# Bias columns to ScalarE, one square sum to VectorE, one sum for half of the first scale, and a new order of all instructions

## The chip, the cores and the metric

The kernel runs on one core of a Trainium2 chip. A core has a matrix engine (PE, TensorE; its weight loads are listed apart as PEld), a vector engine (DVE, VectorE), a scalar engine (ACT, ScalarE), a general engine (POOL, GpSimd) and an engine that issues DMAs (SP, SyncE). Each engine works through a stream of its own in the order in which the program gives it, and waits by semaphores for the others. PE writes its results to PSUM, a memory of eight banks on 128 partitions; DVE and ACT carry them from there to SBUF. The metric is the device time of one execution in microseconds.

## The reference

One layer of a hybrid decoder, 1024 tokens of width 1024, all in float32. What the change touches is marked.

- A modulation vector `c` gives shift, scale and gate columns: `silu(c) @ w_mod + b_mod`. The first **scale** multiplies the normalized `x` before the input projection.
- One input projection `x_mod @ w_in` gives q, k, v, z of four heads (128 columns each) and the inputs lx and gates ly of the recurrent group (four tiles of 128 columns each). The shift enters as a bias: a **column** `shift @ w_in` is added to every token.
- The heads run a chunked gated delta rule: a triangular system per chunk of 64 tokens is solved, then a state is carried from chunk to chunk.
- The recurrent group convolves lx, makes two gates from it (`r`, `i`), then

```
a = exp(8 r log_sigmoid(lam));  b = sqrt(max(1 - a^2, 1e-12)) * (i * x)
h = scan(h = a*h + b);          y = gelu(ly) * h
```

  and `y` is divided by its root mean **square** over the 512 channels of the group.
- Output projection with residual, then an MLP `relu(h @ w_up)^2 @ w_down` with its own norm, scale and shift, and a last norm.

## The kernel before

All matrices that matter for accuracy are split into a high and a low part (names end in `h` and `l`), and a product is three matmuls: high by high, high by low, low by high. A matrix of 1024 x 128 weights is kept as `<name>_w`, split by ACT (CAST to `<name>_wh`) and DVE (difference to `<name>_wl`).

The stages on the time axis of the profile, as the traces of their tiles lie: the first scale, the norm of `x` and the k projection (0 to about 80 us), then the z, q and v projections, which are woven in among the triangular systems (80 to 230), the chunk recurrence of the four heads with the lx and ly projections (180 to 345), the recurrent gates (310 to 414), the output projection (about 385 to 460), the MLP (485 to 1107), and the last norm.

`Proj` makes one projection tile: `third(i)` runs the matmuls of tokens 0 to 511, 512 to 767 or 768 to 1023 into PSUM tiles `<name>_p0`, `_p1` and `_p2`. `_p2` has two columns more, one of which is the bias column of the tile (column 256). That column is copied to `<name>_b` first (line 678), and then ACT empties each third with it as its bias (Identity for q, v, lx; Silu for z; Gelu for ly) into `<name>_st`. `Key` (k0 to k3) is made in another way, and copies its bias column by itself (line 710).

ACT has a table for each family of functions, and an ACT_TABLE_LOAD stands in its stream where the next function needs another one; the wait of the instruction behind it can stand on the load itself.

The triangular systems: `gc` (Gram products, brought into rows by ACT copies) is multiplied on DVE by `bcoef`, which needs `rnk`, a reciprocal root of `ssk` that POOL computes as a power; the product is transposed to `gg`, and 62 DVE steps on `xx` and `ftmp` build the inverse of 32-row blocks. The transposed results `xnc` and `xtc` feed the PE products `it`, `iy`, `iw` and `iz`.

`lru(ct, ...)` is the recurrent group's tile ct: `gate<ct>..` are PE products of the convolved input xr (split to `xrh` by ACT and `xrl` by POOL, for ct 3 by DVE), ACT takes tanh of them (`ta`, `ti`), exp (`aa`), tanh and square (`a2`), DVE multiplies and clips (`ta`), ACT takes the root, DVE scans, multiplies with the gate into `ly<ct>_st`. Its square (`lsq`) is added to `msum` on POOL; after ct 3, PE sums `msum` over partitions (`lrus`), and by way of a DVE transpose, a POOL power and a trip through DRAM (`lnd`, `lrus_b`) the norm comes to `lcm`, which is split to `lch` and `lcl` for the second half of the output projection (`wl`). `wg` is its first half, over the heads; DVE carries its PSUM tiles to `x1`.

What sets the order: the program first records every operation without issuing it. `emit` (lines 323 to 337) then issues them in the order of a table `ORDER` (unpacked from a text at the head of the file), and gives each tile the buffer that a second table, `SLOTS`, names; so line 336 stands for all instructions but the grouped matmuls of line 462. Nothing else orders the streams. SBUF and PSUM tiles are reused under waits that follow from the two tables.

Of the kernel before, what the change touches and what calls it, by code (L numbers as in the profile page):

```python
# [106 lines left out]
def dram_box(ap):  # L107
# [12 lines left out]
    'qo#TL)E!oz1rw7A@7#3r&)>vNyY8X>v;IRC9h`CCf9&{x4hI(eySB}!gscg9wAGjQLp#Um+NUfwio?PV=22Z-~2%|Lu^aJRScWTJ)=p^-$SBvE~&H6%fu^{RWky1^%U'  # L120
    '7_?Q94&IN!WbGaDZ6GSd2A<f4o{>L-L8&D_a(0p?Gq+Finc;3bu{KKT=vrprELyF#L!$yonwMw<b%FL{^yk`%$hi9yktUMYoV3S?Kn*D%Pt^JIs{X0%WUS7Ve<X%cFY'
    'D5f&Ve}Ybdh<Fz$>M|{|Wtzcs!5{(pw!C<IFd<lGNv}p0vT=JtdRAkilZ@etckL0^bkUiLz4LO0wqEsggVNM(T(1i}u$z=|=>Ha&0A<t9^;tY<=$CAy>xASsg;WCdn;'
    '*AMa!W4Ka+=QcmIX66E6weMcT>E555BMyGS$23_iz;IG~!`#*Vh)DD)4G6qYB$OV0jFIq|;KD|N)p4L?%s{`{u&I@%u3u?GH6r>REWd2*?6z<P768qzcmM0tZB|b{U2'
    'CMCK1qg`3KjC0HRULXF7&Tcl<Ld-6FFUhrBBOK+mdwO6{k)%pb$z?G`5s?u+BoQG8b-5ZvjrC}NB_tEQq0%L)Zjp`1ep<m7voH3*=?Kq$WOtJ7dlS{YfqicyuQHh^my'
    'w!?2thlfW?OY8K<gtF(Go;p4H6e$N#cd4Y<XUB@X$s!EjO8WX1$jr5@ibw(pvw`a;7&_xI|oxFI9u8~dTzVr!cu?aB-mFpoy^kDVu7^%*g$;)TiCV6@rBy(j8@{Q$=5'
    'N(LCIsWr^6_8s#`PubVZZktYum<VRD5&s;pADEHa%X}FOYCB_On2wfE-@f*G)cZVWBu>kEL0excl1YwPhJ&afW`Vt>MYS)se4<G<(qxeP_PQ)JbL?mtWCwZ+Y%`Npmf'
    'OX6^(PY}U)fCB&4hygql}+LGU!d27MyGDOImeo=yI^HU2I<XT#`rx2iXPK)6o_(jbxQg(Kg=Y;BjqZ-qAnJnxNIjUZR%Q1$GN(?~;$~Pw-+hFw$I_g5G}S9Cx@JTrP('
# [1670 lines left out]
```

## Time and profile before

| | |
|---|---|
| median of 3 runs | 1121.72 us (1120.87 to 1121.75) |
| the profiled execution | 1120.65 us, its span 1118.9 us |
| PE busy | 1099.6 us (98% of the span) |
| DVE, ACT, POOL busy | 821.6, 599.4, 229.4 us |
| ACT table loads | 24, 1.28 us each |
| granted TensorE clock, mean | 0.997 |

Rows of a timeline read: start in us, duration, engine, line, operation, output and inputs with the tile numbers left out, shapes, and in brackets the idle time of that engine before it and what ended it. Rows of the windows give a stretch, its length, busy time and number of instructions of PE, PEld, DVE, ACT and POOL, then the granted clock, the DMA engines' busy share and GB/s. Rows of waits: who waited for whom, us in total, times, the longest.

### The profile page before, as it was taken

The numbers are of one execution on the slowest core, as the hardware profiler recorded it, in microseconds if no ns is written. First come the engines' busy times: TensorE is split into PE (matmuls) and PEld (weight loads), VectorE is DVE, ScalarE is ACT, GpSimd is POOL, SyncE is SP. The second block draws the span as 40 slices with busy tenths as digits, with TensorE's granted clock in tenths as the row PEclk, the third lists the DMA queues.
The fourth block names the chain that finished last, engine by engine and source line by source line (L and its number), as shares of the span: only waits on it lengthen the run. The fifth ranks groups of instructions, "written<-read, shape, count | busy, mean of one in ns | idle before, by whom it ended". The sixth has DMA issues, their size and how long they took to land.

```text
span 1118.9 us, 16315 instructions
## 1 busy us (share of the span) xinstructions
PE 1099.6 (98%) x6146; PEld 915.9 (82%) x6146; DVE 821.6 (73%) x1116; ACT 599.4 (54%) x917; POOL 229.4 (21%) x149
## 2 busy tenths in 40 slices
PE   9999999999999989999999999999999999999997
PEld 8799898998888767778888878777888888888886
DVE  5789986968998766899767877776493565565663
ACT  5749344545299852467544544555753443531633
POOL 1000200110102322000113032240500365812021
PEclk9999999999999999999999999999999999999999
DMA  9946716657872762440789898888999987848213
GB/s 338 312 138 239 253 44 215 199 209 270 312 255 77 189 186 77 151 151 1 270 293 313 280 332 305 290 267 294 383 319 351 357 263 248 323 154 288 69 38 132
DMA packets 167785, 256.96 MB, mean 230 GB/s; under 512 B 44485, under 2 KB 88986, under 8 KB 167706
## 3 DMA queue, kind: packets, MB, share of 16 engines
q1 hardware_dynamic: 167466, 255.69, 67.8%
q8 instruction: 48, 0.79, 0.3%
q14 instruction: 31, 0.25, 0.1%
q10 hardware_dynamic: 240, 0.23, 0.1%
HBM read 186.63 MB, written 69.25 MB: 229 GB/s over the span
## 4 chain that ended last, share of the span: by engine, by line
PE 58%; DVE 1%; issue 1%; DMA 0%; ACT 0%; POOL 0%; POOLq 0%; DVEq 0%; ACTq 0%
PE dn L336 27%; PE upx L336 15%; PE upz L336 8%; PE wl L336 4%; PE upy L336 4%; DVE U L336 0%; DMA wd<-in_w_down_dram 0%; DVE as L336 0%; DVE lcm L336 0%; POOL lcl L336 0%; DVE x L336 0%; ACT act L336 0%; DVE act L336 0%; DVE wu L336 0%; PE n2b L336 0%
## 5 line engine op out<-in xcount | busy, mean ns | idle before, releaser
L336 PE MATMUL upx<-h2h,U 128*128 128x512 f32 x512 | 166.9, 395 | 0.5 <-DVE U L336 0.5
L336 PEld LDWEIGHTS upx<-h2h,U 128*128 128x128 f32 x512 | 96.0, 188 | 24.2 <-DVE U L336 1.0
L336 ACT CAST U<-wu 128x512 fp32r<-128x512 f32 x112 | 66.6, 617 | 54.1 <-DVE wu L336 13.5
L336 POOL TENSOR_TENSOR wd<-wd,wd 128x512 f32<-128x512 f32 x32 | 47.2, 1482 | 234.9 <-DMA wd<-in_w_down_dram 90.7
L336 PE MATMUL upx<-h2l,U 128*128 128x512 f32 x256 | 93.6, 395 | 0.0
L336 DVE TENSOR_TENSOR U<-wu,U 128x512 fp32r<-128x512 f32 x112 | 79.9, 737 | 15.3 <-ACT U L336 14.9
L336 PE MATMUL upz<-h2h,U 128*128 128x512 f32 x256 | 89.0, 394 | 0.0
L336 ACT ACTIVATE act<-act 128x512 f32<-128x512 f32 x112 | 68.0, 629 | 27.3 <-DVE act L336 26.5
L336 PEld LDWEIGHTS upz<-h2h,U 128*128 128x128 f32 x256 | 48.0, 188 | 11.4
L336 PEld LDWEIGHTS upx<-h2l,U 128*128 128x128 f32 x256 | 48.1, 188 | 11.1
L336 ACT COPY ek<-upx 128x512 f32<-128x512 f32 x48 | 28.0, 584 | 48.9 <-PE upx L336 48.4
L336 PE MATMUL upz<-h2l,U 128*128 128x512 f32 x128 | 47.4, 394 | 0.0
L336 PE MATMUL upy<-h2h,U 128*128 128x512 f32 x128 | 47.0, 395 | 0.2 <-DVE U L336 0.2
L336 DVE TENSOR_TENSOR act<-upz,ek 128x512 f32<-128x512 f32 x32 | 21.9, 688 | 33.6 <-PE upz L336 26.2
L336 POOL TENSOR_TENSOR R<-R,R_5o 128x1024 f32<-128x1024 f32 x8 | 21.8, 2730 | 90.1 <-DMA R_5o<-in_w_down_dram 82.1
L336 DVE TENSOR_TENSOR wu<-wu,wu 128x512 f32<-128x512 f32 x48 | 36.1, 758 | 0.2
L336 ACT ACT_TABLE_LOAD x24 | 30.8, 1283 | 8.2 <-DVE bcoef L336 5.6
L336 ACT ACTIVATE vn<-ch,bcoef 128x128 f32<-128x128 f32 x32 | 11.8, 368 | 38.8 <-PE ch L336 38.8
L336 PE MATMUL v_p<-hh,v_wh 128*128 128x256 f32 (+2 forms) x96 | 30.0, 334 | 2.1 <-ACT z_st L336 2.1
L336 DVE TENSOR_TENSOR R_5l<-R,R_5h 128x1024 fp32r<-128x1024 f32 x8 | 15.1, 1891 | 21.5 <-PE dn L336 16.8
L336 PE MATMUL v_p<-hh,v_wl 128*128 128x256 f32 (+2 forms) x96 | 29.9, 337 | 0.0
L336 PE MATMUL v_p<-hl,v_wh 128*128 128x512 f32 (+2 forms) x96 | 29.7, 338 | 0.0
(601 smaller groups left out, 3372.2 us busy)
## 6 DMA issues: line engine op xcount, KB each, us to landing
L<-aod SPq DMA_DIRECT2D x56, 512.0 KB, 7.1
R<-in_w_down_dram SPq DMA_DIRECT2D x40, 512.0 KB, 5.2
wu<-in_w_up_dram SPq DMA_DIRECT2D x32, 512.0 KB, 4.7
aod<-as SPq DMA_DIRECT2D x64, 256.0 KB, 5.6
wd<-in_w_down_dram SPq DMA_DIRECT2D x32, 512.0 KB, 5.1
aod<-act SPq DMA_DIRECT2D x48, 256.0 KB, 2.8
sc_w<-in_w_mod_dram SPq DMA_DIRECT2D x16, 512.0 KB, 8.1
sh_w<-in_w_mod_dram SPq DMA_DIRECT2D x16, 512.0 KB, 11.2
```

What stands on the lines that cost most here:

```text
L336: op.fn(*[res(v) for v in op.a], **{n: res(v) for n, v in op.k.items()})
```

## The change

- `Proj.third`: the bias column of the 20 tiles z, q, v, lx, ly is copied by ACT and not by DVE.
- `scale1(2)`, which makes four of the eight columns of the first scale: one weighted sum over all eight blocks of `w_mod` (one ACT product, seven DVE steps of 128x512, four one-column matmuls) in place of two sums over four (two products, six steps, eight matmuls).
- `lru`: for ct 3 the square is added to `msum` on DVE; ct 1 and 2 stay on POOL.
- Both tables are new: `ORDER` and `SLOTS` differ from the first entry to the last, on all engines.

```diff
@@ Proj.third
                 self.b = small(f"{self.name}_b", 1)
-                V.tensor_copy(self.b, p[:, 256:257])
+                A.copy(self.b, p[:, 256:257])
@@ scale1
-        for a in range(0 if q == 2 else 2, 2):
-            acc = big(f"sc1_acc{q}{a}")[:, 0:w]
-            for k in range(4):
-                wt, c = sc1_w[q, (4 * a + k) // m][:, (4 * a + k) % m, :], cact[:, 4 * a + k:4 * a + k + 1]
+        if q == 2:
+            acc = big(f"sc1_acc{q}")[:, 0:w]
+            for k in range(NK):
+                wt, c = sc1_w[q, k // m][:, k % m, :], cact[:, k:k + 1]
                 if k == 0:
                     A.mul(acc, wt, c)
                 else:
                     V.scalar_tensor_tensor(out=acc, in0=wt, scalar=c, in1=acc, op0=ALU.mult, op1=ALU.add)
             for j in range(n):
-                mm(pc[:, j:j + 1], acc[:, j * P:(j + 1) * P], ones[:, 0:1], a == 0 and j == 0, a == 1, skip_group_check=True)
+                mm(pc[:, j:j + 1], acc[:, j * P:(j + 1) * P], ones[:, 0:1])
@@ lru
-            G.tensor_tensor(out=msum, in0=msum, in1=sq, op=ALU.add)
+            (V if ct == 3 else G).tensor_tensor(out=msum, in0=msum, in1=sq, op=ALU.add)
@@ the tables
 _ORDER = (
-    'c-nQF2b5Js)2^%c1ZIE%hMXCqLmo0nkR*si1q2ZRQIIG}K#-gyN0B5TC?bkV5JYlNkc{M<b7o+M3Fma(r?=nz{&m;7|6(yG?7e$eSH1PtTfO_l$uTV^nIu(%Y9vI$B*'
+    'c-noN2Y6N0v-W50lL7%k2tD*3s?s|mAkq{>5fDKIM0ynn9YlH+qzNc0sDKC}BE6$@=`Hl$AxKTmS@ZqYmgnC8_uS`Rc#@o)v-euFX5M+{owasE!o~c@{~UZ>RU`lZ|D'
...
```

Three places in the new order. First ACT at the z projections; `p0`, `p1`, `p2` are the thirds of a tile, `st` its result, `b` its bias column. Before:

```order
L336 CAST v0_wh_1435<-v0_w_690 128x1024 [waits DMAHW2_49]
L336 CAST q1_wh_1446<-q1_w_1273 128x1024 [waits DMAHW2_49,DMAHW0_49]
L336 ACT_TABLE_LOAD [waits DVE_49]
L336 ACTIVATE z1_st_1567<-z1_p2_1162,z1_b_1530 128x256 [waits PE_49]
L336 ACTIVATE z1_st_1567<-z1_p1_1353,z1_b_1530 128x256 [waits PE_49]
L336 ACTIVATE z1_st_1567<-z1_p0_1142,z1_b_1530 128x512 [waits PE_49]
```

And with the change:

```order
L334 CAST q1_wh_1462<-q1_w_841 128x1024
L334 COPY gc_1333<-LT_1193 32x256 x2
L334 COPY z2_b_1505<-z2_p2_1359 128x1 [waits PE_49]
L334 ACT_TABLE_LOAD [waits PE_49]
L334 ACTIVATE z2_st_1522<-z2_p0_1211,z2_b_1505 128x512 [waits Activation_49]
L334 ACTIVATE z2_st_1522<-z2_p1_1341,z2_b_1505 128x256
L334 COPY z1_b_1587<-z1_p2_1155 128x1 [waits PE_49]
L334 ACTIVATE z1_st_1594<-z1_p0_1187,z1_b_1587 128x512 [waits PE_49,Activation_49]
```

z2 is emptied ahead of z1, its bias comes from ACT itself, and the table load waits for PE where it waited for DVE.

Second, ACT from the exp of the recurrent gates of ct 2 to the evacuations of ly3. Before:

```order
L336 ACT_TABLE_LOAD
L336 ACTIVATE aa2_4307<-ta2_4243,nc2_1222 128x1024 [waits Activation_49]
L336 ACTIVATE wo5h_4309<-wo5_4202,cols_570 128x1024 [waits DMAHW2_49,DMAHW1_49]
L336 CAST xrh3_4311<-xr3_4184 128x1024 [waits DVE_49,PE_49]
L336 ACTIVATE ta2_4243<-ta2_4243,c2_880 128x1024 [waits Activation_49]
L336 CAST gch01_4160<-gcm3_4317 128x512 [waits DMAHW3_49]
L336 ACTIVATE a22_4321<-aa2_4307 128x1024
L336 ACTIVATE ti2_4246<-gate25121_4196,hxb_3071 64x512
L336 ACT_TABLE_LOAD
L336 ACTIVATE ta2_4243<-ta2_4243 128x1024 [waits DVE_49]
L336 ACT_TABLE_LOAD [waits DVE_49]
L336 ACTIVATE ly3_st_4355<-ly3_p2_4213,ly3_b_4353 128x256 [waits Activation_49]
```

With the change:

```order
L334 ACTIVATE aa2_4320<-ta2_4206,nc2_1170 128x1024 [waits Activation_49]
L334 ACTIVATE ti2_4218<-gate25120_4198,hxb_2972 64x512
L334 ACTIVATE a22_4328<-aa2_4320 128x1024 [waits PE_49,Activation_49]
L334 ACTIVATE ta2_4206<-ta2_4206,c2_964 128x1024
L334 ACTIVATE ti2_4218<-gate25121_4200,hxb_2972 64x512
L334 CAST xrh3_4336<-xr3_4181 128x1024
L334 CAST gch01_4126<-gcm3_4313 128x512 [waits DMAHW3_49]
L334 ACT_TABLE_LOAD
L334 ACTIVATE ta2_4206<-ta2_4206 128x1024 [waits DVE_49]
L334 COPY ly3_b_4341<-ly3_p2_4187 128x1 [waits PE_49]
L334 ACT_TABLE_LOAD
L334 ACTIVATE ly2_st_4133<-ly2_p1_4108,ly2_b_4095 128x256 [waits PE_49]
```

The square a22 moved up behind aa2, other work of ACT down to just ahead of the root, and an evacuation of ly2 down behind the root.

Third, DVE from the clipping of ta3 to the transpose of lrus. Before:

```order
L336 SCALAR_TENSOR_TENSOR ta3_4386<-a23_4445,ta3_4386 128x1024 [waits Activation_49]
L336 TENSOR_SCALAR ta3_4386<-ta3_4386 128x1024 [waits DVE_49]
L336 SCALAR_TENSOR_TENSOR x1_000_4473<-wg00_4423,g1_2785,xT00_4327 128x512 [waits DMAHW6_49,PE_49]
L336 TENSOR_TENSOR xr3_4184<-xr3_4184,ta3_4386 128x1024 [waits Activation_49]
L336 SCALAR_TENSOR_TENSOR xr3_4184<-aa3_4407,xr3_4184 128x1024 [waits DVE_49]
L336 TENSOR_TENSOR ly3_st_4355<-ly3_st_4355,xr3_4184 128x1024 [waits DVE_49]
L336 TENSOR_TENSOR gcl11_4476<-gcm3_4317,gch11_4384 128x512 [waits DMAHW3_49,Activation_49]
L336 SCALAR_TENSOR_TENSOR x1_101_4538<-wg50_4430,g1_2785,xT20_4331 128x512 [waits DVE_49,DMAHW0_49,PE_49,Pool_49]
```

With the change:

```order
L334 SCALAR_TENSOR_TENSOR ta3_4369<-a23_4443,ta3_4369 128x1024 [waits Activation_49]
L334 TENSOR_SCALAR ta3_4369<-ta3_4369 128x1024 [waits DVE_49]
L334 SCALAR_TENSOR_TENSOR xr3_4181<-ti3_4381,xr3_4181 128x1024 [waits Activation_49]
L334 TENSOR_TENSOR xr3_4181<-xr3_4181,ta3_4369 128x1024 [waits DVE_49,Activation_49]
L334 SCALAR_TENSOR_TENSOR xr3_4181<-aa3_4441,xr3_4181 128x1024 [waits DVE_49]
L334 TENSOR_TENSOR ly3_st_4363<-ly3_st_4363,xr3_4181 128x1024 [waits DVE_49]
L334 SCALAR_TENSOR_TENSOR x1_000_4449<-wg00_4411,g1_2778,xT00_4519 128x512 [waits DMAHW5_49,PE_49]
L334 TENSOR_TENSOR msum_4128<-msum_4128,lsq3_4536 128x1024 [waits Activation_49,Pool_49]
L334 TENSOR_TENSOR gcl11_4436<-gcm3_4313,gch11_4366 128x512 [waits DMAHW3_49]
```

The evacuation of wg00 moved behind the scan and the gate product, and the last addition to msum follows it on DVE.

More of the change, by code (lines that the diff above doesn't have):

```diff
@@ L120 @@
[L120 to L127, printed above, removed]
@@ new lines @@
+    'Rkf&G{WWI}B@mP!V{>!phi^*C2cic<*T&=z)yVb33D{HuCV@#3_lhTq;^2!A5Bpdu|E68*IXBtT-k2I5btoj1)td;!CY9vnFiWcgp(nH^o9a>T5O0rGniZDrS!X?S3G'
+    'Y@TNN!FcOLk{tIW!a>U@LQsGmEX9oiA=&Djd(YT`%B6xea2NudLH}MaZe@*$P(6&pOwd9-Br!$d#4#+i8@*PN(bG@>t9*l3T@07ndOFt$v~N}XEfgTSGa`mPJk6eNk;'
+    'iZzvB9UAHV!so7eOCN{6Seb8WH~kXB;xPgb+uda{|=L`Vr4jXi1PCYJ9bim_6K=oICi4l>WTx;$QArS%wTJ1ZzJ_ZY!QdReXor6<<i!lv7-BQ+ik!#k(3b+L|MZRxou'
+    'f|x$CwLG`7zP2LYtH_s({VU!MmmXNBx($#2u8mmDF@44N!9)FAhsfvJgY~V^x3KjujgY<)$ttp$i`K<DNtfu`vPMhDpIV97s;<@~y)6U4$#LDlO79S(e)uASYh%rQ+c'
@@ new lines @@
+    '<1MN*4UHPSSGS5LPiqOM?s}lR(OA+>?j*&PX#|g3ZNcnbeZQ`l*hVLAq6{>oh4P*G<h(Ojr}W9(3996F7OuI^(r2qfC~{tUX%#fYrqsLsmTDv!I3;wH@}&B}yTEsM+w'
+    'c!*4k2d7=-9<!dqyRKF(WGz}ThOD1?9YU@x*t{Na0bQAYim0$QiO4jQoys}GA>hAx_!~masEQ|R5RMRq|%gu-6Ul`un2(k^fN8pc1<U}eg2&u;vK|iy)=oj+3#OPe`_'
+    '(W4<RVre3P4DS?t;tpQG&|TxOJtUK%R;Znr)HAf%KbH7%zZM@A{Zs<b*MkvbME#SIfB)m<+rE0T;IUjn(~9R)I?ceOPTk<PlTM4L$)dR&yf~d(MRona!Yaf0L1hQ{r5'
+    'ZbWU(D4-xAHY<%vYI#y|8;`4*pf@`G(<n)}(ji|>Oqqp1z&RFT~_St`jfuwL41wW;Nq3^YdWgdDdRaolp&Y_c8nPaUk6;gEtLxQ}FJ9lwI)G+NOFHG{O*edOL*8^kBK'
@@ new lines @@
+    '$c$@R+dSo-k$Cb??V_*C+pPTuEvcvFxjiK#eS1T?*H$(e&1|@*p{Wce+w<AWM82<FmI<LbW}dw%O|YjtsO_usWD88t%5L-uhi=1B30jBj=*Rp;G`APdx>Dr3&{_FV8='
+    'LMnFZT_Xu6Bf%MYHNr6QL>ck1h{&HP=D1Y6fuB%ibjlqf7zf5FwrMLVxe7me*F?G01zy700zE>zrd#ur7sbJgMjX7TT^^q^Gwj6we&1^cyV$k8aQ=#JsQ^kQ%xJ&$N|'
+    ')Y#Fbp<dVgqTwZbT{xUiC)DF;fdPMr_I(TD`RMO05UMNg5d%xH>%|{^cv^^pBLM6NkS{6nbEyFd1?248$I*#ZJvL9(FqgYl34`+f!uj)(s9cy=}twYA9=oo1zwRDAy('
+    '9-4+d^G{I)+Mhx!dA)J9;V!7N6Gh+SNmz^Kn1T>@Pf{^hm0rRXlpsI%d|PwtTuiaBMHoUS}x(4u@Z&N_a!5~OK*z8vnR;PiH!6w`u>y*u;T(SkSfs6-hx|m$qpi0#jJ'
@@ new lines @@
+    'o4-vxgj*vTx}eO&dGp;*5TyUWPpfDH}=Cv_S5O|#Bkmu#wX9VX4kJAHIB8JeK|ye~u3{fcx7E{P;=o;X}ihRt$$DcalCA@dV7GO*Dm+ZgG@=UidxNkJ)z{cTJsNw7=!'
+    '9@L_Cis@~;n^E|yJr%YUqt&wK%?7*~qo-`V$!E6X%}4rJAK0GS)_ViyYy=Z;)KBCDUc5zY*6BNTr`bbA>kb1w0Oc9r=fAN#qZ|vR2@E3cRdv5K4Mlr%i9i(?BEmXfz2'
+    'Z%yo>i8%cC9Wo@4}$_^d+*U9%zcSHD#QsE<c*~a=~UWzXvm!R_F$W<A;NrqH<KfBCmVfh2|X5j+2V8&w65ZS2J6yyU54_#Q1eE<21)jYUWD37RmooaL5iSNowqkghA5'
+    'CGo47zrlSTImx&r-u7_exq`WW9?PuPwP*MCEh8N%kyqTUF=3ZqW6Q03~QLq5@D73?Trm0Mq&`|RIk~dz;YTHnPiPdsCme|CEB?Q;$M6lb|EDW{rqNSaU#s}rhNt;gk!'
@@ new lines @@
+    '){4L>ykYQ^OcBrDY#5xH3j~eKxR+yk@beRD)i7xANrsA>c9UF2p^k#SI*;q$L0B@1(_Q!zrVPriHVk3RIzmOTWFzv5SAD`?J`*#nC&*wB-?k*O;FZRck*sV)*B`j^)K'
+    '#AVZ8_c&w2mzf1H=BEx2R0ER>I_d+*@a2U-i?A0rBB@P97(RC@7yZt^@v3h7awiK2<h2((OUDv48!Pl=7wP(@(XfXoG<*JM@bqR9gGO6p)Duvow0^JpR-U`-YjSlxg|'
+    'Ne#oe>hdG(V`Qt{C^6*Qc@0SpW;rcWY!-PJrpSW=Nl)~nvFw=+ls9cf69<c&6{jYCw>P-EpjP*J<~cS|@faf&c3;$AYz>oEf71`RJDQ4c7aXj$jTmQ<PBAAmpPaOjlF'
+    'rL!uTaNbHJ?R|3zN<=86DD43`}g$Evd-EL1v^aEBmB3+!7}l?f>rEVfq>0-!%Q<hwpV8Ys~TD>LhYR8Q(G&I@-IeqwOf(nQXfnr@|)N=Q2~v+X~+9P>LQlUEEb6)#F}'
@@ L244 @@
+    'wuze33NMJuDS`Wgjomxt&!_E;KUrI?p(?ECeVuJf`H-yR<9jMv)3hAC{4;q)5Xh==-k2%P0s-3;50`y*&q#bXpJ~9PO;^2*bnjB{!S#>$1P;h|rOjsj1Iedt3I'
 )
```

219 lines of the change are left out of this document (102 added, 117 removed).

## The prediction

> **What bounds the kernel now.** First the page: busy times, then the chain that ended last.
>
> ```profile
> span 1118.9 us, 16315 instructions
> PE 1099.6 (98%) x6146; PEld 915.9 (82%) x6146; DVE 821.6 (73%) x1116; ACT 599.4 (54%) x917; POOL 229.4 (21%) x149
> ```
>
> PE is busy all but 19.3 us, so moving work between ACT, DVE and POOL can only act on those 19.3 us and on the rate of the matmuls. The view of waits, for PE alone, tells what ended the idle time:
>
> ```profile
> PE v_p L336 <- ACT z_st L336: 2.1, 1, 2.1
> PE wg L336 <- DVE x L336: 1.9, 1, 1.9
> PE wl L336 <- ACT lch L336: 1.9, 2, 1.8
> PE wg L336 <- ACT ly_st L336: 1.7, 1, 1.7
> PE lrus L462 <- POOL msum L336: 1.0, 1, 1.0
> PE ly_p L336 <- DVE sc L336: 0.7, 1, 0.7
> ```
>
> These six make 9.3 us; the rest is mostly the start and the last sum and store, which no edit touches. Four lie in 387 to 430 us (the recurrent gates and the output projection), one at 118. That one I read in the timeline of each engine:
>
> ```profile
> 117.57 0.40 PE L336 MATMUL z_p<-hl,z_wh 128*128 128x512 f32 x1
> 120.07 0.39 PE L336 MATMUL v_p<-hh,v_wh 128*128 128x258 f32 x1 [2.10 <-ACT z_st L336]
> 116.24 0.17 DVE L336 TENSOR_TENSOR bcoef<-beta,rnk 128x8 f32<-128x8 f32 x1 [1.16 <-POOL rnk L336]
> 117.74 0.15 DVE L336 COPY z_b<-z_p 128x1 f32<-128x1 f32 x1
> 118.25 1.28 ACT L336 ACT_TABLE_LOAD   x1 [5.61 <-DVE bcoef L336]
> 119.54 1.42 ACT L336 ACTIVATE z_st<-z_p,z_b 128x256 f32<-128x256 f32 x3
> ```
>
> PE wants a PSUM bank of z1. ACT must empty it, needs the bias column first, and that copy stood on DVE behind bcoef, which waited for POOL. ACT was idle 5.61 us and even its table load began only after the copy. The windows view shows a second cost:
>
> ```profile
> 121.50:125.00 3.50, 3.50 (x15) 3.29 (x14) 3.09 (x13) 0.00 (x0) 0.00 (x0) 0.51 0.99 349
> 125.00:128.00 3.00, 3.00 (x21) 2.71 (x20) 2.83 (x11) 0.48 (x1) 0.00 (x0) 1.00 0.27 78
> ```
>
> The column before the DMA share is the granted clock: 0.51 for 3.5 us after the stall, so (1 - 0.51) x 3.5 = 1.7 us more. The place costs 2.1 + 1.7 = 3.8 us. The idle times of 1.9 and 1.7 us had no such drop behind them.
>
> **The change part by part.** All against the profiled run, 1120.65 us (span 1118.9), which lies 1.07 below the median 1121.72.
>
> *Bias columns.* Twenty DVE copies of 0.15 us (117.74) become ACT copies. No such copy is on ACT before; the nearest row is ACT's smallest operation:
>
> ```profile
> L336 ACT ACTIVATE first<-ones 128x1 f32<-128x1 f32 x1 | 0.2, 202 | 0.0
> 360.00:400.00 40.00, 38.23 (x214) 31.44 (x214) 28.74 (x26) 35.80 (x45) 9.21 (x4) 1.00 0.76 202
> ```
>
> Bounds 0.15 (DVE's price) and 0.4 us; I take 0.2, so ACT gains 4 us in all. ACT sat free for 5.6 us at 118, but is busy 35.8 of 40 us in 360 to 400: eight copies lie ahead of or in that stretch.
>
> *z stage (A).* The copies no longer stand behind bcoef: -3.8. But in the new order the table load waits for PE, for the last matmul of the bank z2_p0. The same bank is wanted by q0_p1 after eight matmuls of 256 columns and one of 512, about 1.3 us (125 to 128 has 21 of both kinds in 3.0 us, 0.14 each). The last matmul's own 0.40 (117.57), the load's 1.28 and an evacuation of 0.7 (estimated from 119.54, 1.42 for three) make 2.4: a new wait of 1.1 us (bounds 0 and 2.1). Behind it stands the triangular inverse, one long DVE chain that feeds `it`:
>
> ```profile
> 155.89 1.38 DVE L336 COPY LT<-xtc 32x1024 f32<-32x1024 f32 x2
> 158.59 1.20 PE L462 MATMUL it<-xnc,LT 32*32 32x32 f32 x64
> 107.40 0.43 DVE L336 TENSOR_TENSOR sq<-gc,id 128x256 f32<-128x256 f32 x1 [0.54 <-ACT gc L336]
> 108.24 0.69 DVE L336 TENSOR_TENSOR LT<-kk,k_dm 128x512 f32<-128x512 f32 x1 [0.42 <-ACT k_dm L336]
> ```
>
> DVE ended at 157.27, PE arrived 1.3 us later without a wait. PE now comes 3.8 - 1.1 = 2.7 earlier, and by the order has about 1.2 us fewer matmuls ahead of `it`: it would stand there 2.7 + 1.2 - 1.3 = 2.6 us before DVE's old time. DVE gains what it no longer waits: the 1.16 at bcoef (now three other operations and ktl stand between) and some 0.5 of less work; the 0.54 and 0.42 may stay. I take a wait of 1.0 at `it` (bounds 0 and 2.6). A = -3.8 + 1.1 + 1.0 = -1.7.
>
> *lx and ly (B).* The ly wait for a bias copy behind scale 2's sum goes:
>
> ```profile
> 284.13 0.47 PE L336 MATMUL ly_p<-hh,ly_wh 128*128 128x512 f32 x1 [0.68 <-DVE sc L336]
> 309.89 1.28 ACT L336 ACT_TABLE_LOAD   x1
> 311.18 1.42 ACT L336 ACTIVATE ly_st<-ly_p,ly_b 128x256 f32<-128x256 f32 x3
> ```
>
> -0.7. Before, the load at 309.89 started ahead of what it serves. Now ly1's load waits for PE as z2's does, and gate100 wants that bank 1.15 us of matmuls later: 1.28 + 0.5 + 0.4 - 1.15 = 1.0. ly0's load follows its bias copy, with a bank wanted 1.2 us after its last matmul; the load has a head start of about a us, so 0.5. B = +0.8 (bounds -0.7 and +2).
>
> *Recurrent stage (C).* The chain of rows that ends in lrus:
>
> ```profile
> 375.45 1.28 ACT L336 ACT_TABLE_LOAD   x1
> 384.69 1.66 DVE L336 TENSOR_SCALAR ta<-ta 128x1024 f32<-128x1024 f32 x1
> 386.39 1.06 ACT L336 ACTIVATE ta<-ta 128x1024 f32<-128x1024 f32 x1 [1.80 <-DVE ta L336]
> 395.80 1.28 ACT L336 ACT_TABLE_LOAD   x1
> 402.43 2.76 DVE L336 TENSOR_SCALAR ta<-ta 128x1024 f32<-128x1024 f32 x1
> 405.23 1.06 ACT L336 ACTIVATE ta<-ta 128x1024 f32<-128x1024 f32 x1 [1.84 <-DVE ta L336]
> 409.91 1.23 DVE L336 TENSOR_TENSOR ly_st<-ly_st,xr 128x1024 f32<-128x1024 f32 x1
> 411.23 1.06 ACT L336 ACTIVATE lsq<-ly_st 128x1024 f32<-128x1024 f32 x1 [3.38 <-DVE ly_st L336]
> 412.43 2.38 POOL L336 TENSOR_TENSOR msum<-msum,lsq 128x1024 f32<-128x1024 f32 x1 [7.78 <-ACT lsq L336]
> 414.86 0.64 PE L462 MATMUL lrus<-msum,ones 128*32 128x256 f32 x8 [1.04 <-POOL msum L336]
> ```
>
> In the new order ta2's square stands right behind aa2, with xrh3 and a gch cast moved after it, so DVE's work is done when ACT reaches the square root: -1.8. Between that root and the load at 395.80 ACT gets one ly2 evacuation and one bias copy: +0.4. For ct 3 two ACT operations (ti3, lsq2) change places around the root, and lsq2 behind it means that POOL's msum no longer runs beside the DVE maximum (402.43; the one of ct 2, beside less, took 1.66 at 384.69): of load to end of root, 10.5 us, I count 8.5: -2.0. The last msum on DVE, priced by 409.91, saves 2.38 - 1.23 = -1.2. Together -4.6; PE has 0.9 us fewer matmuls ahead of lrus, so PE gains 3.7. gate301 will wait some 1.4 us for a ly2 bank that ACT empties only after the root; that lies inside this chain and is not added. Bounds 0 (another engine late) and -4.6. DVE takes msum behind a PSUM evacuation and ahead of a gcl and the lrus transpose; the transpose waits for lrus anyway. C = -3.7.
>
> *From lrus to lch (D).*
>
> ```profile
> 421.14 0.33 SPq L336 DMA_DIRECT2D lrus_b<-lnd  x1
> 427.82 2.36 DVE L336 TENSOR_TENSOR lcm<-lcm,lrus_b 128x1024 f32<-128x1024 f32 x2 [3.27 <-DMA lrus_b<-lnd]
> 429.75 0.73 PE L336 MATMUL wl<-lch,wo0h 128*128 128x512 f32 x2 [1.75 <-ACT lch L336]
> ```
>
> lrus_b took 6.7 us behind weight loads. In the new order three wo loads come earlier, while lrud<-ly3_st and one lcm load now stand behind lnd on SP; PE has 0.7 us more to do meanwhile. D = -1.0 (bounds -1.75 and +1).
>
> *First scale.* One ACT product and four one-column matmuls go, one DVE step comes:
>
> ```profile
> L336 DVE SCALAR_TENSOR_TENSOR sc_acc<-sc_w,cact,sc_acc 128x512 f32<-128x512 f32 x6 | 4.4, 750 | 0.1
> 29.02 0.16 DVE L336 SCALAR_TENSOR_TENSOR A<-bcol,sc_c 128x4 f32<-128x4 f32 x1 [1.16 <-PE sc_c L336]
> ```
>
> The k projection's matmuls hide it, since PE waits for nothing there, and DVE waited 1.16 itself; without cover it costs one step, 0.75. I take 0.
>
> *Small waits (E).* A new order makes some that I cannot see: one more like that at 284.13, +0.7.
>
> Sum: -1.7 + 0.8 - 3.7 - 1.0 + 0.7 = -4.9, so 1121.7 - 4.9 = **1116.8 us** as a median.
>
> [...] The granted clock fell after an idle time of 2.10 us. [...]
>
> **The rivals.**
>
> *Inverse swallows the gain.* DVE's chain to `it` stays as late as it was; PE waits 2.6 there instead of 1.0. For it: DVE is busy without a break from 116 to 157, so an earlier PE does not hurry it. Against: its waits ahead of 116 shrink. +1.6: 1118.4.
>
> *ACT sets the pace in 320 to 400.* Eight bias copies (1.6 us, lx and ly) and two more table loads (2.6, as 375.45) fill the 4.2 us that ACT had free, so the tanh, exp and root chain arrives no earlier and C is 0. For: 35.8 of 40 us. Against: 3.6 us of ACT's waiting (386.39, 405.23) goes too. +3.7: 1120.5.
>
> *Table loads behind PE halve the clock.* The slower side: a load that waits for the last matmul of a bank wanted at once. From 1 us of further lateness of ACT on, the idle time reaches the 2.1 us after which the clock fell, and z2, ly0 and ly1 cost 3.8 each instead of 1.1, 0.5 and 1.0: +8.8, less the 1.0 at `it`: +2.9 against before, 1124.6. For: the same mechanism at 120.07. Against: idle ACT at 112 to 118, and 1.9 us of idle time that did nothing.
>
> *The clock drop comes again elsewhere* (its phase, not that stall, decides): +1.7, 1118.5.
>
> That the edit doesn't do what it says is no rival: the order shows every copy on ACT.
>
> **How the numbers follow.** Forecast 0.42, inverse 0.15, ACT 0.18, table loads 0.15, clock 0.10. The best ends of the bounds (no wait at `it` 1.0, C 0.9, D 0.75, no new ly waits 1.5, no E 0.7, half of z2's 0.5) are 5.3 below the forecast: 1111.5. Above, the ACT case and part of the table-load case: 1122.5. A measurement of this kernel tells about 0.2% (2.2 us) from no change. Faster: nine tenths of the forecast, two thirds of inverse and clock, a quarter of ACT: 0.58. Slower: two thirds of the table-load case and a little of ACT and forecast: 0.15. Same: 0.27.
>
> **What would show it.** Right: no clock below 0.9 behind 118; the wait v_p<-z_st gone and one of about 1 us of q_p on z_st; `it` waiting for DVE 0 to 2; gate waits on ly_st of about 1 us at 305 to 345; roots of ta without waits; lrus 4 us earlier, waiting for DVE. Wrong: a wait above 2 us with half clock behind it, gates waiting for xrh or xrl, or new waits ahead of 100 us or among the chunks of 180 to 340.

## The result, and the profile after

The changed kernel takes 1110.9 us (median; 1109.87 to 1112.11) against 1121.3 for the kernel before: a ratio of 0.9909, 95% interval 0.9892 to 0.9926. Forecast were 1116.8 us: the direction held, the gain of 10.4 us is twice the 4.9 of the sum, and the time lies below the range's lower end of 1111.5. The profiled run took 1110.3 us, 10.35 less than that of before.

The page of the changed kernel, its span and its engines:

```profile
span 1108.5 us, 16288 instructions
PE 1095.2 (99%) x6138; PEld 913.6 (82%) x6138; DVE 800.0 (72%) x1098; ACT 604.2 (55%) x938; POOL 216.1 (19%) x148
```

PE's idle time fell from 19.3 to 13.3 us, so 6.0 us of the gain were waits. The other 4.4 are PE's busy time (1099.6 to 1095.2): 1.7 of half clock at 121.5 us, about 0.6 for the four one-column matmuls that went (eight rows in the trace), and some 2 us in pieces too small to name. DVE is busy 21.6 us less with nearly the same work. The waits of PE in the changed kernel (total, count, longest):

```profile
PE lrus L460 <- DVE msum L334: 2.0, 1, 2.0
...
PE q_p L334 <- ACT z_st L334: 1.0, 1, 1.0
PE gate L460 <- ACT ly_st L334: 0.9, 1, 0.9
PE wl L334 <- ACT lch L334: 0.6, 2, 0.4
...
PE gate L460 <- ACT lx_st L334: 0.4, 1, 0.4
```

Gone are both waits at wg (1.9 and 1.7), that at ly_p, 1.3 of the 1.9 us at lch, and those for U among the up products. The new q_p and ly_st waits are the forecast table loads. The wait at lrus has grown from 1.0 to 2.0 us.

To put sizes on the terms I set, in each kernel, the time at which PE stands at a place against the sum of the median pitches (start to start) of the matmuls ahead of it. The table has the difference between the kernels, place by place, good to about 0.2 us:

| term | forecast | measured |
|---|---|---|
| A: z stage and `it` | -1.7 | -2.5 |
| B: lx, ly and the chunks, to about 367 us | +0.8 | -1.6 |
| C: gates to lrus | -3.7 | -2.5 |
| D: lrus to lch | -1.0 | -2.0 |
| E: small waits; measured are those among the up products | +0.7 | -1.25 |
| first scale and k projection, with eight matmul rows fewer | 0 | -0.6 |
| sum | -4.9 | -10.4 |

For C and D three pieces of the engines' timelines tell most. Of before, the scan of ct 3 and the row's little root step, with the VectorE product beside it:

```profile
407.58 2.29 DVE L336 TENSOR_TENSOR_SCAN xr<-aa,xr 128x1024 f32<-128x1024 f32 x1
...
416.21 1.28 DVE L336 SCALAR_TENSOR_TENSOR wo2l<-wo,cols,wo2h 128x1024 fp32r<-128x1024 f32 x1
...
416.37 2.62 POOL L336 TENSOR_TENSOR lrus_r<-lrus_r,mhalf 128x8 f32<-128x8 f32 x1 [1.57 <-DVE lrus_r L336]
```

Of after, the same scan, now beside GpSimd's addition, and the same root step, now alone; then the row's DMA and its user:

```profile
398.84 2.54 POOL L334 TENSOR_TENSOR msum<-msum,lsq 128x1024 f32<-128x1024 f32 x1 [17.84 <-ACT lsq L334]
399.15 4.38 DVE L334 TENSOR_TENSOR_SCAN xr<-aa,xr 128x1024 f32<-128x1024 f32 x1
408.87 1.65 POOL L334 TENSOR_TENSOR lrus_r<-lrus_r,mhalf 128x8 f32<-128x8 f32 x1 [7.48 <-DVE lrus_r L334]
...
412.75 0.56 SPq L334 DMA_DIRECT2D lrus_b<-lnd  x1
...
419.55 2.36 DVE L334 TENSOR_TENSOR lcm<-lcm,lrus_b 128x1024 f32<-128x1024 f32 x2 [0.75 <-DMA lrus_b<-lnd]
```

GpSimd beside VectorE was taken off the maximum (2.76 us before) and put on the scan (2.29 to 4.38). The root step lost its neighbour and 0.97 us. The row's way from issue to use is 6.8 us, as before (6.7).

### The profile page after: what moved, and what is told of

It is laid out like the page before. It is cut to its first block, busy times and chain, and to the rows that moved or that the text cites. A ratio compares the mean times of both kernels' runs of the same rounds, so it can differ in the third digit from the quotient of the medians.

```text
span 1108.5 us, 16288 instructions
## 1 busy us (share of the span) xinstructions
PE 1095.2 (99%) x6138; PEld 913.6 (82%) x6138; DVE 800.0 (72%) x1098; ACT 604.2 (55%) x938; POOL 216.1 (19%) x148
## 4 chain that ended last, share of the span: by engine, by line
PE 88%; ACT 5%; DVE 3%; issue 2%; DMA 1%; POOL 0%; SPq 0%; POOLq 0%; ACTq 0%; DVEq 0%
PE dn L334 28%; PE upx L334 16%; PE upz L334 8%; PE wl L334 4%; PE k_p L334 4%; PE upy L334 4%; PE v_p L334 4%; PE q_p L334 4%; PE z_p L334 4%; PE lx_p L334 3%; PE ly_p L334 2%; PE ch L334 2%; PE cho L334 1%; ACT ta L334 1%; DVE xr L334 1%
## 5 line engine op out<-in xcount | busy, mean ns | idle before, releaser
L334 PE MATMUL upx<-h2h,U 128*128 128x512 f32 x512 | 170.3, 395 | 0.0
L334 POOL TENSOR_TENSOR wd<-wd,wd 128x512 f32<-128x512 f32 x32 | 43.9, 1378 | 242.1 <-DMA wd<-in_w_down_dram 123.8
L334 POOL TENSOR_TENSOR R<-R,R_5o 128x1024 f32<-128x1024 f32 x8 | 19.3, 2412 | 91.0 <-DVE L_6l L334 74.2
L334 DVE TENSOR_TENSOR wu<-wu,wu 128x512 f32<-128x512 f32 x48 | 33.0, 701 | 3.2 <-DMA wu<-in_w_up_dram 3.0
L334 PE MATMUL v_p<-hh,v_wh 128*128 128x258 f32 (+2 forms) x96 | 30.4, 338 | 0.0
L334 PE MATMUL q_p<-hh,q_wh 128*128 128x256 f32 (+2 forms) x96 | 28.6, 329 | 1.0 <-ACT z_st L334 1.0
L334 PE MATMUL v_p<-hh,v_wl 128*128 128x258 f32 (+2 forms) x96 | 29.1, 336 | 0.0
```

The source lines that it names most:

```text
L334: op.fn(*[res(v) for v in op.a], **{n: res(v) for n, v in op.k.items()})
```

## Experiments

Theory 1: the new order gives the gain, and the engine of an operation little. Theory 2 (the prediction's reading): the copies' engine gives most at the z stage, the addition's engine a part at lrus. Theory 3 came with the traces: VectorE and GpSimd slow each other (the scan of ct 3 took 4.38 us beside GpSimd's addition, 2.29 without it), and the new order parts them.

### One edit at a time, in the old and in the new order

The bias columns on ScalarE in the old order:

```diff
-                V.tensor_copy(self.b, p[:, 256:257])
+                A.copy(self.b, p[:, 256:257])
```

> The kernel before with one edit: the bias columns leave PSUM by ScalarE; order and everything else as before. Theory 1 (the new order gives most of the gain, the engine of the copies little): the z bank's table load still follows the last matmul of z1 (copy 117.74 to 117.89 on VectorE, load 118.25; on ScalarE the copy would end at about 118.15), so the wait of 2.10 us and the half clock behind it stay; only the wait of 0.68 us at ly_p goes: -0.7 us, between -1.5 and 0. Theory 2 (the prediction's reading: the copy stood behind bcoef on VectorE): the 2.10 us and the 1.7 us of half clock go, -3.8 us, and -0.7 at ly_p, in all -4.5, less up to 2 us if the triangular inverse's wait then appears at `it`: -2.5 to -4.5.

1121.88 us against 1120.29: ratio 1.001 (1.0 to 1.0019), no gain. Its waits of PE:

```profile
PE upy L336 <- DVE U L336: 1.3, 1, 1.3
PE gate L462 <- ACT ly_st L336: 1.0, 1, 1.0
...
PE kk L336 <- ACT z_st L336: 1.0, 1, 1.0
PE gate L462 <- ACT ti L336: 0.9, 1, 0.9
PE ly_p L336 <- DVE sc L336: 0.7, 1, 0.7
PE v_p L336 <- ACT z_st L336: 0.6, 1, 0.6
```

Both theories missed a part. The wait of 2.10 us fell to 0.60 and no half clock followed (mean granted clock 0.998; 0.997 before), so theory 2 reads the z stage rightly. But ScalarE's other work now stands behind copies that wait for PE, and PE got new waits at kk and twice at the gates. The z stage's gain is given back there: PE is 1.0 us ahead of the kernel before at `it` and 1.3 behind it at lrus. The 1.3 instead of 0.2 us at the up products is not the edit's doing; the run with the sum of eight in the old order has the same 1.3, with the copies on VectorE.

The wait of 0.7 at ly_p stayed too, which the prediction and both theories gave to a bias copy. In the trace of before PE waits there for `sc`, behind a step `rso` that took 0.92 us beside a GpSimd operation; its shortest time in that trace is 0.15:

```profile
280.95 2.41 POOL L336 TENSOR_TENSOR q3T<-q3T,q_gb 128x1024 f32<-128x1024 f32 x1 [21.48 <-ACT qs L336]
282.47 0.92 DVE L336 TENSOR_SCALAR rso<-on_w 128x8 f32<-128x8 f32 x1
...
283.90 0.15 DVE L336 TENSOR_TENSOR sc<-sc_c,bcol 128x8 f32<-128x8 f32 x1
```

So it is the new order, and not the copies' engine, that takes this wait away.

The same edit undone in the new order:

```diff
-                A.copy(self.b, p[:, 256:257])
+                V.tensor_copy(self.b, p[:, 256:257])
```

> The changed kernel with one edit undone: the bias columns leave PSUM by VectorE again, in the new order. Theory 1 (order): the time moves by less than 1.5 us, since the table loads follow the matmuls in both: +0.3 to +1.5 (the copy now crosses from VectorE to ScalarE by a semaphore, some 0.2 us at each of five table-load places, and stands behind 1 to 4 us of VectorE's queue at a few). Theory 2 (the copies' engine gives most): +5 us and more, with the wait of 2 us and the half clock back at 118 us.

1146.4 us, ratio 1.0228 (1.0211 to 1.0245): 35 us above the changed kernel. First from its timelines, then the start of the same chain in the changed kernel:

```profile
125.09 0.16 DVE L334 COPY z_b<-z_p 128x1 f32<-128x1 f32 x1 [1.89 <-PE z_p L334]
...
129.01 0.21 DVE L334 TENSOR_TENSOR ftmp<-gg,xx 128x31 f32<-128x31 f32 x1
...
135.84 0.15 DVE L334 COPY q_b<-q_p 128x1 f32<-128x1 f32 x1
...
136.56 0.80 PE L334 MATMUL z_p<-hh,z_wh 128*128 128x256 f32 x2 [6.03 <-ACT q_st L334]
...
168.76 1.45 PE L460 MATMUL it<-xnc,LT 32*32 32x32 f32 x47 [6.13 <-DVE xnc L334]
```

```profile
119.63 0.21 DVE L334 TENSOR_TENSOR ftmp<-gg,xx 128x31 f32<-128x31 f32 x1
...
151.37 1.38 DVE L334 COPY LT<-xtc 32x1024 f32<-32x1024 f32 x2
```

A copy of one column ahead of the inverse waits for PE and holds VectorE's whole chain back by 9.4 us; another inside the chain makes ScalarE, then PE, wait for the chain. These places make PE about 14 us late at `it`; some 16 more come among the lx and ly projections (the longest wait there is 3.9 us for VectorE's lx_wl) and were not taken apart. Neither theory had this: this order cannot be had with the copies on VectorE. In the new order the edit's worth is that it lets the inverse stand early and unbroken (152.7 instead of 157.3 us at its end), more than the copies' own wait.

The addition of ct 3 to msum on VectorE in the old order:

```diff
-            G.tensor_tensor(out=msum, in0=msum, in1=sq, op=ALU.add)
+            (V if ct == 3 else G).tensor_tensor(out=msum, in0=msum, in1=sq, op=ALU.add)
```

> The kernel before with one edit: the last addition to msum (ct 3) on VectorE instead of GpSimd; order as before. The prediction's price: 2.38 - 1.23 = -1.15 us in the chain to lrus. In the old order VectorE's queue holds other work around 412 us, which takes the addition late at worst by one step of about 1.2 us: so -1.2 if VectorE is free, 0 if not. If PE, which waited 1.04 us at lrus, has nothing else late, no more than 1.04 can come back there: -1.0. The rest of the chain's 2.5 us (recurrent stage) and the 2.0 us behind it must then be the order's.

Ratio 1.0011 (1.0002 to 1.002), nothing gained, as expected where VectorE's queue is in the way: the addition begins at 413.73 instead of 412.43 us and ends 0.14 us later than GpSimd's. In the new order the same edit undone:

```diff
-            (V if ct == 3 else G).tensor_tensor(out=msum, in0=msum, in1=sq, op=ALU.add)
+            G.tensor_tensor(out=msum, in0=msum, in1=sq, op=ALU.add)
```

> The changed kernel with one edit undone: the last addition to msum on GpSimd again, in the new order. GpSimd's addition took 2.38 us before against 1.22 on VectorE after, at the place where PE waits 1.97 us for it: +1.2 us at lrus, and as much at the end if lrus is on the path. If VectorE, which is free of the addition, ends the scan or what follows earlier, less: +0.6. A time within 0.3 us of the changed kernel's would mean that the addition's engine is off the path.

1111.4 us, ratio 0.9918 (0.9904 to 0.9933). The wait at lrus is 3.0 instead of 2.0 us, and PE is 1.1 us later there; at the end the median differs from the changed kernel's by 0.5, which two ratios with these intervals do not tell apart.

One sum of eight for half of the first scale, in the old order:

```diff
-        for a in range(0 if q == 2 else 2, 2):
-            acc = big(f"sc1_acc{q}{a}")[:, 0:w]
-            for k in range(4):
+        if q == 2:
+            acc = big(f"sc1_acc{q}")[:, 0:w]
+            for k in range(NK):
```

> The kernel before with one edit: one running sum of eight instead of two of four for the upper half of the first scale (one ScalarE product and four one-column matmuls fewer, one VectorE step of 0.75 us more), everything else in the old order. The prediction's price is 0: the k projection's matmuls hide it. The PE's own work falls by four matmuls of one column, some 0.3 us at most: -0.3 to 0. If VectorE's added step makes bcol and A late, +0.75.

1120.63 against 1119.82 us, ratio 1.0006 (0.9997 to 1.0016): by the time nothing, by the trace not free. PE waits, and the windows (length, busy PE, PEld, DVE, ACT, POOL, granted clock, DMA) show half clock behind it:

```profile
28.68 1.17 PE L340 MATMUL sc_c<-ones,sc_acc 128*128 128x1 f32 x8 [1.35 <-DVE sc_acc L340]
```

```profile
29.50:32.80 3.30, 3.30 (x11) 2.58 (x12) 1.65 (x4) 2.36 (x4) 0.00 (x0) 0.50 0.87 262
```

PE is 2.3 us behind the kernel before at the end of the k projection, but only 0.5 at `it`, as the wait at the z stage had no half clock behind it in this execution (mean granted clock 0.997 in both, here with the stretch above and before with that at 121.5 us). In the changed kernel the same matmuls start without a wait at 28.22 us: there the order has put VectorE's last step before PE's arrival. So each of the three edits alone brings nothing in the old order, and the gain comes with the new one. That the new order needs an edit is shown for the bias columns alone: the addition undone cost little, and the sum of eight was not undone. The two tables, `ORDER` and `SLOTS`, were not tried apart.

### What is left: table loads and the scan

Spare operations of one column on ScalarE start the Silu and Gelu tables ahead of z2 and ly1 (their results are used by nothing):

```diff
+ORDER.insert(ORDER.index(1218), 8009)
+ORDER.insert(ORDER.index(2854), 8010)
+    spare = small("spare", 1)
+    A.activation(spare, triu[:, 0:1], AF.Silu)
+    A.activation(spare, triu[:, 0:1], AF.Gelu_apprx_tanh)
```

> The changed kernel with two spare operations on ScalarE (one column each, not used by the result): a Silu ahead of the bias copy of z2 and a Gelu ahead of the evacuation of ly1, so that the table loads begin before the bank's last matmul instead of behind it. If those two loads are what PE waits for at q_p (1.04 us) and at gate100 (0.88 us), both waits go and the time falls by 1.5 to 1.9 us, to about 1109.0. If the waits fall but the recurrent chain, which ends at lrus in a wait for VectorE, takes the second one back, -1.0. If the loads were not the cause (the evacuations themselves), the waits stay at 0.7 or more each and the time moves by less than 0.4 us.

1108.63 us, ratio 0.9899 (0.9879 to 0.9919). Both waits (1.04 us at q_p, 0.88 at gate100) are gone: what PE waited for were the loads. PE leads by 2.3 us behind gate100. At lrus a wait of 1.92 us stays, and in the profiled execution half clock followed it (mean granted clock 0.996; 0.999 with both edits, below).

The addition of ct 2 to msum moved to VectorE, ahead of that of ct 3:

```diff
+ORDER.remove(3071)
+ORDER.insert(ORDER.index(3259), 3071)
-            (V if ct == 3 else G).tensor_tensor(out=msum, in0=msum, in1=sq, op=ALU.add)
+            (V if ct >= 2 else G).tensor_tensor(out=msum, in0=msum, in1=sq, op=ALU.add)
```

> The changed kernel with GpSimd's addition to msum of ct 2 moved to VectorE, right ahead of that of ct 3, so that nothing runs on GpSimd beside the scan of ct 3. Theory: the scan took 4.38 us there against 2.29 before because GpSimd's addition ran beside it (398.84 to 401.38); alone it takes 2.3 us, and VectorE reaches the last addition 2.1 us earlier less 1.2 us for the added addition: the wait of 1.97 us at lrus falls to about 1, the time by 0.9 us (0.5 to 1.5). Rival: the scan is long for another reason (its input arrives in parts, or the two semaphores): then it stays above 4 us and the added addition makes the time 1.2 us longer.

```profile
399.02 2.29 DVE L336 TENSOR_TENSOR_SCAN xr<-aa,xr 128x1024 f32<-128x1024 f32 x1
...
406.70 0.64 PE L462 MATMUL lrus<-msum,ones 128*32 128x256 f32 x8 [1.32 <-DVE msum L336]
```

With GpSimd idle the scan takes 2.29 us. PE leads by 0.7 us behind lrus; 1109.38 us, ratio 0.9907 (0.9885 to 0.993), is too near the changed kernel to tell. Both edits together:

> The edits of the early table loads and of the clear scan together. If the two act at different places, their gains add: -1.5 and -0.9, about 1108.4 us. If the early loads' gain at ly1 is swallowed at lrus, the sum is larger here than the two alone, since the scan's shortening then gives room: also about -2.4. If neither theory holds, the time stays at 1110.9 or above.

1107.59 us (0.9889; 0.9871 to 0.9908). This version and the unedited changed kernel were then run on one chip:

> The changed kernel without any edit, on the same chip as the run that follows: 1110 to 1111 us, 0.991 of the kernel before.

> The changed kernel with the early table loads and the clear scan, on the same chip as the changed kernel. By the traces PE loses 1.04 at q_p, 0.88 at gate100 and 0.65 at lrus less, 2.6 us in all, and 3.0 with the smaller waits: -2.6 us (-2.0 to -3.3).

1110.91 us (0.9923; 0.9909 to 0.9937) and 1107.18 us (0.989; 0.9877 to 0.9904): 3.7 us less, the best version here, and more than the 3.3 that were expected at most. The three waits that were shortened account for 2.6 us; most of the rest is in the trace of the changed kernel itself, where this time half clock followed the wait at lrus:

```profile
407.16 0.64 PE L460 MATMUL lrus<-msum,ones 128*32 128x256 f32 x8 [1.93 <-DVE msum L334]
```

```profile
408.10:411.40 3.30, 3.30 (x9) 2.64 (x8) 0.82 (x3) 0.00 (x0) 1.65 (x1) 0.50 0.00 0
```

### VectorE beside GpSimd

In the old order, the addition of ct 2 moved off the maximum of ct 3:

```diff
+ORDER.remove(3075)
+ORDER.insert(ORDER.index(3260) + 1, 3075)
-            G.tensor_tensor(out=msum, in0=msum, in1=sq, op=ALU.add)
+            (V if ct == 2 else G).tensor_tensor(out=msum, in0=msum, in1=sq, op=ALU.add)
```

> The kernel before, old order, with one addition moved: that of ct 2 to msum from GpSimd (402.23, beside VectorE's maximum) to VectorE behind the last product of ct 3, where VectorE is free while ScalarE squares. Theory 3 (VectorE and GpSimd slow each other where they run side by side, and the new order's gain from 330 to 440 us is largely that it parts them): the maximum takes 0.7 instead of 2.76 us, the root starts 1.8 us earlier, PE's wait of 1.92 us at 403.6 for VectorE's x falls to 0 to 0.2, lrus starts 1.8 us earlier: -1.8 us (-1.0 to -2.1). Rival (the maximum is long for its data, or PE's wait at 403.6 has another end): the wait stays, within 0.4 us of before.

and, in a second kernel, wo2l moved behind the row's root step as well:

```diff
+ORDER.remove(3497)
+ORDER.insert(ORDER.index(3268) + 1, 3497)
```

> The same, and VectorE's product wo2l, which ran beside GpSimd's little root step (lrus_r, 416.37, 2.62 us; 1.65 in the changed kernel, where wo2l stands behind the step), moved behind the second transpose of the row. Theory 3: GpSimd's step takes 1.65 us, the row is sent 1.0 us earlier and PE's wait of 1.75 us at 429 for lch falls to about 0.8: 1.0 us less than with the first edit alone, -2.8 against before. Rival (the weight loads ahead of the row's DMA set its landing, as the prediction had it): the row lands at the same time, no difference to the run with the first edit alone.

1117.97 us (0.9986; 0.9976 to 0.9995) and 1117.22 us (0.9977; 0.9968 to 0.9987) against 1119.59. Of the kernel before, GpSimd's addition beside the maximum (2.76 us from 402.43); then the first kernel's maximum, then the second's root step and the row's user:

```profile
402.23 2.42 POOL L336 TENSOR_TENSOR msum<-msum,lsq 128x1024 f32<-128x1024 f32 x1 [16.43 <-ACT lsq L336]
```

```profile
402.31 0.69 DVE L338 TENSOR_SCALAR ta<-ta 128x1024 f32<-128x1024 f32 x1
```

```profile
414.70 1.65 POOL L340 TENSOR_TENSOR lrus_r<-lrus_r,mhalf 128x8 f32<-128x8 f32 x1 [1.56 <-DVE lrus_r L340]
...
425.17 2.36 DVE L340 TENSOR_TENSOR lcm<-lcm,lrus_b 128x1024 f32<-128x1024 f32 x2 [0.86 <-DMA lrus_b<-lnd]
```

Theory 3 holds at both places. The maximum took 0.69 instead of 2.76 us, the wait of 1.92 us for x, which ended at 405.91, went, and PE leads by 2.2 us there and by 1.7 behind lrus (1.57 of wait remain). With wo2l moved the step takes 1.65 us, and PE's wait at lch falls from 1.87 in the first kernel to 0.75; the medians differ by 0.75 us, with intervals that overlap. No weight load was moved: about 1.0 of the 2.0 us in D is the neighbour of an eight-column step (2.62 us beside it, 1.65 without), not the DMA queue.

Six additions of the down weights moved to VectorE, behind the steps they ran beside:

```diff
-        G.tensor_tensor(out=b12, in0=b22, in1=b12, op=ALU.subtract)
+        (V if n in (10, 11) else G).tensor_tensor(out=b12, in0=b22, in1=b12, op=ALU.subtract)
...
+for _i, _j in ((5759, 5782), (5760, 5759), (5761, 5760), (5895, 5832), (5896, 5895), (5897, 5896)):
+    ORDER.remove(_i)
+    ORDER.insert(ORDER.index(_j) + 1, _i)
```

> The kernel before, old order, with six additions of the down weights (wd10 and wd11, at 737.9 to 742.9 and 748.7 to 753.4 us) moved from GpSimd to VectorE, each three behind the two or three steps of VectorE that they ran beside (U of 738.28, 3.48 us for two; wu and U of 748.75, 5.24 for three). Theory 3 (the waits among the up products, 0.21 and 0.52 us in the trace of before, are of VectorE slowed by GpSimd): the two U take 1.3, wu and U 2.0 us, both waits go: -0.7 us, up to -1.8 in executions in which the waits are longer (1.28 and 0.47 us with the bias columns on ScalarE). Rival (VectorE has too much to do there, whatever runs beside): the six additions' 4.1 us on VectorE make the waits longer, +0.5 and more.

Of before, PE's waits at these places, and the two U with the first of GpSimd's additions:

```profile
PE upx L336 <- DVE U L336: 0.5, 1, 0.5
...
PE upy L336 <- DVE U L336: 0.2, 1, 0.2
```

```profile
737.89 1.62 POOL L336 TENSOR_TENSOR wd<-wd,wd 128x512 f32<-128x512 f32 x1 [8.85 <-DVE as L336]
738.28 3.48 DVE L336 TENSOR_TENSOR U<-wu,U 128x512 fp32r<-128x512 f32 x2
```

Of this kernel, the two U and one of the additions, now on VectorE:

```profile
737.31 1.28 DVE L339 TENSOR_TENSOR U<-wu,U 128x512 fp32r<-128x512 f32 x2
738.52 0.68 DVE L339 TENSOR_TENSOR wd<-wd,wd 128x512 f32<-128x512 f32 x1
```

The two U take 1.28 instead of 3.48 us. Both waits of PE are gone although VectorE does six operations more, and across this place PE gains 1.2 us on the kernel before. The time does not show it: 1119.53 us, ratio 1.0001 (0.9992 to 1.001). One trace explains why: in the run with maximum and root step clear, where nothing was changed at this place, neither wait is there, the two U took 2.39 us, and PE gains as much. When the additions run, and so what they stand beside, varies between executions of the old order: its wait for U at upy was 1.3, 0.2 or none. That the additions make the two U long is shown; that this edit takes away more than such a variation is not.

### A longer wait at z2

Nine, and in another kernel thirteen, spare Silu operations of 128 columns ahead of the first evacuation of z2 (one line each, used by nothing):

```diff
+ORDER.insert(ORDER.index(1244), 8009)
+    spare = small("spare", 128)
+    A.activation(spare, triu[:, 0:128], AF.Silu)
```

> The changed kernel with nine spare operations on ScalarE (not used by the result) between the z stage's table load and the first evacuation of z2, so that PE's wait at q_p grows from 1.04 to about 2.1 us. Theory (the gain of the z stage reaches the end): +1.1 us, 1.7 more in the executions in which the granted clock falls. Rival (an earlier z stage is swallowed further on, at `it` or at lrus, as in the run with the bias columns moved in the old order): within 0.5 us of the changed kernel. The clock: in the ten traces so far it was granted at half for 3.41 us only after a stretch of a fixed grid of 3.41 us in which PE idled 1.92 us or more (apart from stretches with very short matmuls or already at half clock), and never after 1.81 us or less; a wait of 2.1 us then brings the drop only where nearly all of it lies in one stretch of the grid, so in about half of the executions. [...]

> The same with thirteen spare operations: a wait of about 3.3 us at q_p, 2.3 us more than in the changed kernel. If the z stage's gain reaches the end: +2.3, and 1.7 more with the clock drop, +4.0 (2.0 to 4.3). If it is swallowed: below +1. [...]

1112.61 us (0.9935; 0.9921 to 0.995) and 1115.35 us (0.9957; 0.9941 to 0.9974). Of the first, the wait and the window behind it; of the second, the same, and the window behind lrus:

```profile
123.54 0.58 PE L343 MATMUL q_p<-hh,q_wh 128*128 128x256 f32 x1 [2.46 <-ACT z_st L343]
```

```profile
123.30:126.60 3.30, 3.06 (x14) 3.06 (x15) 3.13 (x8) 0.55 (x2) 0.00 (x0) 0.50 1.06 379
```

```profile
124.24 0.58 PE L347 MATMUL q_p<-hh,q_wh 128*128 128x256 f32 x1 [3.83 <-ACT z_st L347]
```

```profile
123.60:130.30 6.70, 6.06 (x27) 5.97 (x28) 6.29 (x17) 0.95 (x3) 0.00 (x0) 0.50 0.91 298
...
413.70:417.00 3.30, 3.30 (x9) 2.53 (x9) 1.00 (x3) 0.00 (x0) 1.65 (x1) 0.50 0.00 0
```

The profiled span grew by 3.3 us in the first. PE is 0.4 us late ahead of the z stage, 3.2 at `it` and 3.3 at lrus and at the end: 1.4 of wait and 1.4 of clock, with nothing taken back. In the second it grew by 6.3: PE is 5.2 us late at `it` (2.8 of wait, the rest two stretches at half clock, the first of which it began still waiting), 5.5 at lrus, 7.1 behind a third stretch at half clock there, and 6.3 at the end, as its wait at lch shrinks. So what the z stage loses in the changed kernel reaches the end. The other way holds too: with the early table loads PE came to `it` 1.2 us earlier and still did not wait. The rival of an inverse that swallows the gain falls for this order.

## Why the prediction was right in direction and wrong in size

The gain is 5.5 us larger than the sum. B brought 2.4 more than forecast, E 1.95, D 1.0, A 0.8 and the first scale with its matmuls 0.6; C brought 1.2 less. That the direction came out rests on A and C, whose mechanisms were there; B and E were forecast as losses and came out as gains, and half of D came for another reason than the one given, which was luck.

**A.** The wait that went (3.8) and the one that came (1.1; 1.04 measured) were as forecast. The step that failed is "I take a wait of 1.0 at `it`": there is none. VectorE was priced to gain 1.16 + 0.5 us; it ended the inverse 4.5 earlier (152.7 for 157.3), as the chain starts 2.1 us earlier and less stands between its steps; PE comes to `it` at 155.0, 2.3 us behind VectorE. The inverse rival falls with it.

**B.** The load at ly1 costs 0.9, as forecast at 1.0. The 0.5 at ly0 did not come, and a wait of 0.4 for lx_st did. The ly_p wait went (0.7), but "The ly wait for a bias copy behind scale 2's sum goes" has the wrong cause: PE waited for `sc` behind a step beside GpSimd, and moving the copies alone left the wait. The step that failed is the sum of +0.8. The waits about cancel (0.6 at iw went as well, 0.5 at ch came), and what the sum put at nothing gave about 1.7 us: many losses of under 0.4 us each between matmuls of different kinds. All seven traces of the old order have them, so they belong to the order; no run took them apart, and their cause is open.

**C.** "Together -4.6" counted that GpSimd's addition leaves the maximum, but not that it comes to stand beside the scan: +2.1 on VectorE, and a wait of 2.0 us at lrus. Clearing the scan gave 0.7 of it back. The size was wrong, the chain right.

**D.** The step "lrus_b took 6.7 us behind weight loads" failed as a reason. It took 6.8 in the new order, with none issued in the 20 us ahead of it; 1.0 us of the gain was the root step's neighbour, shown by moving wo2l alone. For the other 1.0 the 0.7 us of PE work that the order puts ahead of lch is one candidate; that was not tried apart.

**First scale.** "I take 0" holds in the new order. The price without cover was put at 0.75; the trace in the old order shows a wait of 1.35 us and half clock.

**E.** "A new order makes some that I cannot see: +0.7" had the wrong sign: -1.25. It counted new small waits and no old ones that go; the two for U, 0.2 and 0.5 us, were in the trace of before, and the prediction never looked at the up products. The other 0.5 there are small losses that were not taken apart. The size holds for this pair of executions alone: one trace of the old order has no wait for U, two have 1.3 us at upy, and none of the ten of the new order has any.

**The rivals.** ScalarE does not set the pace: its roots of ta run without a wait and both waits at wg are gone. Table loads do cost what they were given at z2 and ly1 (1.04 and 0.88 us, with full clock behind them in the changed kernel). The clock drop does come again elsewhere, at lrus, in some executions (the changed kernel's second trace, the early loads, the thirteen spare operations). What no rival held is that GpSimd beside VectorE is a cost which the order moves about: clearing it took away the wait of 1.9 us at wg and half of D, and by the rows it made those at ly_p (0.7) and for U (0.2 and 0.5). It was in the quoted row of 2.76 against 1.66 us, used once and not carried on.

## What to carry to other kernels

A new order cannot be priced edit by edit: three edits that each bring nothing in the old order came to 10 us with the new one, and the new one without the bias columns' move lost 26 against the kernel before. For every VectorE step on a critical chain, read what GpSimd does in the same microseconds, before and after; a step that takes two to six times its usual time is the mark of it (here 4.38 for 2.29 us, 2.76 for 0.69, 0.92 for 0.15). Two waits of PE behind a table load (1.04 and 0.88 us) went when a one-column operation of the same function was placed earlier.
